# A gradient kernel at the DMA ceiling: scheduler semaphores in place of a critical section, and the last two stores on the queue of the loads

## Chip, cores, metric

One core of a Trainium2 chip. The metric is device time in microseconds of the whole program. The kernel before takes 1248.62 us (median of three runs, 1247.94 to 1251.06).

## The reference

```python
# x: float32 [8192, 8192]
np.gradient(x, axis=1)
# inside a row: (x[j+1] - x[j-1]) / 2 ; at its two ends: x[1]-x[0] and x[m-1]-x[m-2]
```

268.44 MB are read and 268.44 MB written, with one subtraction and one halving per element.

## The kernel before

Rows are handled in 32 sets of 256 (128 partitions times two rows, 8.39 MB). Three slots hold a set each. A set is loaded 64 columns to the right of where its result goes, so that one VectorE pass can work in place. GpSimd first puts the four row-end values aside; the pass covers 16382 columns; a small copy places the row ends; a store sends the set out.

```python
with tc.tile_critical():            # all semaphores by hand
    ...
    def load(i):
        k = i % NB
        if i >= NB:
            nc.sync.wait_ge(ld[(i - 1) % NB], 16 * ld_n[(i - 1) % NB])   # load before has landed
            nc.sync.wait_ge(st[k], 16 * st_n[k])                         # slot has been stored
        nc.sync.dma_start(out=slots[k][:, SH : SH + W], in_=x_sets[i]).then_inc(ld[k], 16)
    ...
    for i in range(nsets):
        at = put_aside(i)                                   # GpSimd
        if i < nsets - 1:
            at = halve(b, 1, W - 1, at)                     # VectorE, 16382 columns
            at = place(nc.scalar if i % 2 else nc.vector, ...)
            store(nc.scalar, i, 0, W, at, st[k])            # ACT queue
        else:                                               # last set in four quarters
            for q in range(PIECES):
                at = halve(b, c0 + 1 - right, c1 - right, at)
                put = place(nc.scalar, ...)
                store(nc.sync, i, c0, c1, put, st_last[q])  # SP queue
        if i + NB < nsets:
            load(i + NB)
    # ... SP waits for all stores
```

## Time and profile before

| what | kernel before |
|---|---|
| median time | 1248.62 us |
| span of the profiled run | 1247.0 us |
| VectorE busy | 554.4 us, 44% |
| bytes and mean rate | 536.88 MB, 431 GB/s |
| last load: issued, landed | 1177.1, 1216.1 us |

How to read it: the page gives the span, the busy time of each engine, the share of DMA engines in use in 40 slices and the chain that ended last. "Stretches" are rows of start:end in us, length, busy time of each engine (number of instructions), the TensorE clock, DMA share, GB/s. The *period* is the mean distance between load issues from the seventh load (near 209 us) to the last, 25 steps; 16.78 MB at the ceiling of 434.3 GB/s take 38.63 us. *Lost DMA time* is worked out from the packet records: the bytes of each packet are spread over its duration, and what is missing from 434.3 GB/s is turned into microseconds, a mean over the 16 engines. The lines of the page, the stretches and the timeline are shown in the prediction.

### The profile page before, as it was taken

The numbers are of one execution on the slowest core, as the hardware profiler recorded it, in microseconds if no ns is written. First come the engines' busy times: TensorE is split into PE (matmuls) and PEld (weight loads), VectorE is DVE, ScalarE is ACT, GpSimd is POOL, SyncE is SP. The second block draws the span as 40 slices with busy tenths as digits, with TensorE's granted clock in tenths as the row PEclk, the third lists the DMA queues.
The fourth block names the chain that finished last, engine by engine and source line by source line (L and its number), as shares of the span: only waits on it lengthen the run. The fifth ranks groups of instructions, "written<-read, shape, count | busy, mean of one in ns | idle before, by whom it ended". The sixth has DMA issues, their size and how long they took to land.

```text
span 1247.0 us, 259 instructions
## 1 busy us (share of the span) xinstructions
DVE 554.4 (44%) x51; ACT 5.0 (0%) x20; POOL 6.5 (1%) x36
## 2 busy tenths in 40 slices
DVE  2841552355533555334553345533455433554335
ACT  0000000000000000000000000000000000000000
POOL 0000000000000000000000000000000000000000
DMA  9999999999999999999999999999999999999998
GB/s 404 437 435 435 412 431 437 435 437 437 437 431 435 435 431 423 435 435 437 433 435 437 437 437 433 431 423 433 435 435 437 435 437 433 435 423 437 435 418 360
DMA packets 9649, 536.88 MB, mean 431 GB/s; under 512 B 1072, under 2 KB 1072, under 8 KB 1072
## 3 DMA queue, kind: packets, MB, share of 16 engines
q1 hardware_dynamic: 5184, 276.83, 51.6%
q10 hardware_dynamic: 4464, 260.05, 48.1%
q14 instruction: 1, 0.01, 0.0%
HBM read 268.44 MB, written 268.44 MB: 431 GB/s over the span
## 4 chain that ended last, share of the span: by engine, by line
DMA 96%; DVE 3%; issue 0%; POOL 0%; ACT 0%; SPq 0%
DMA slot<-in_x_dram 93%; DMA out_dram<-slot 3%; DVE slot L90 3%; POOL ends L78 0%; ACT slot L104 0%; DVE slot L104 0%; SPq L163 0%; SPq L68 0%; SPq L44 0%
## 5 line engine op out<-in xcount | busy, mean ns | idle before, releaser
L90 DVE CUSTOM_DVE_ANT_0 slot<-slot 128x16382 f32<-128x16382 f32 (+1 forms) x35 | 551.6, 15761 | 679.2 <-POOL ends L78 679.1
L78 POOL TENSOR_TENSOR ends<-slot 128x4 f32<-128x4 f32 x32 | 6.3, 198 | 1209.6 <-DMA slot<-in_x_dram 1209.6
L104 ACT COPY slot<-ends 128x4 f32<-128x4 f32 (+1 forms) x19 | 3.7, 197 | 1188.4 <-DVE slot L90 1188.4
L104 DVE COPY slot<-ends 128x4 f32<-128x4 f32 x16 | 2.7, 172 | 0.5
L104 ACT ACT_TABLE_LOAD x1 | 1.3, 1283 | 41.0 <-DVE slot L104 41.0
L152 POOL MEMSET const-uint8-127<- 128x1 uint8 x1 | 0.1, 102 | 0.0
L152 POOL MEMSET const-bfloat16-1.0<- 128x1 bf16 x1 | 0.1, 101 | 0.0
L152 POOL MEMSET const-float32-0.0<- 128x1 f32 x1 | 0.1, 98 | 0.2 <-issue 0.2
L152 POOL MEMSET const-float32-1.0<- 128x1 f32 x1 | 0.1, 98 | 0.0
## 6 DMA issues: line engine op xcount, KB each, us to landing
out_dram<-slot SPq DMA_DIRECT2D x4, 2048.0 KB, 10.1
slot<-in_x_dram SPq DMA_DIRECT2D x32, 38.6
out_dram<-slot ACTq DMA_DIRECT2D x31, 37.8
```

The source lines that it names most:

```text
L78: nc.gpsimd.tensor_sub(out=ends[:, i, :, :], in0=xin[:, :, 1 : m : m - 2], in1=xin[:, :, 0 : m - 1 : m - 2],),
L90: nc.vector._custom_dve(dve_ops.TENSOR_TENSOR_REDUCE_SUB_MAX, out=b[:, c0:c1], in0=b[:, SH + c0 + 1 : SH + c1 + 1], in1=b[:, SH + c0 - 1 : ...
L104: return done(copy(out=out, in_=in_), placed[engine])
L152: nc = _bacc.Bacc("TRN2", target_bir_lowering=False, num_devices=1)
```

## The change

Its intent is that the scheduler sets the semaphores (in program order, with dependences dropped that another wait implies), that the placing copies leave ACT, and that the end runs on one queue: the store of the last set but one goes to SP behind the last load, and the last set goes out in two halves instead of four quarters.

```diff
-    with tc.tile_critical():
-        ld = [nc.alloc_semaphore(f"ld{k}") for k in range(NB)]
-        ... (st, st_last, aside, halved, placed, and their counts)
+    def chain(i, ins, *needed):
+        group, engine = f"slot{i % NB}", ins.ins.engine
+        keep = [o.ins for o in needed]
+        ...
+        tc.declare_no_dep(ins.ins, group=group, keep=keep, reason="implied by the needed step")
+    def load(i):
+        ins = nc.sync.dma_start(out=b[:, SH : SH + W], in_=x_sets[i])
+        if i >= NB:
+            tc.add_manual_dep(ins.ins, loads[-1].ins.name, landed, reason="queue empty")
+        loads.append(chain(i, ins, *([stores[i - NB]] if i >= NB else [])))
+    with tc.manual_schedule():
 ...
-                at = place(nc.scalar if i % 2 else nc.vector, ...)
-                store(nc.scalar, i, 0, W, at, st[k])
-            else:
-                step = W // PIECES                       # four quarters
+            nr = 1 if last else R                        # last set: one row at a time
+            for r in range(0, R, nr):
+                ...
+                placer = nc.gpsimd if i % 5 in (1, 3) and not last else nc.vector
+                queue = nc.scalar if i < nsets - 2 else nc.sync
```

## The prediction

> **What bounds the kernel now.** I read the page first: busy shares, the DMA row in 40 slices, and the chain that ended last.
>
> ```profile
> span 1247.0 us, 259 instructions
> DVE 554.4 (44%) x51; ACT 5.0 (0%) x20; POOL 6.5 (1%) x36
> ...
> DMA  9999999999999999999999999999999999999998
> GB/s 404 437 435 435 412 431 437 435 437 437 437 431 435 435 431 423 435 435 437 433 435 437 437 437 433 431 423 433 435 435 437 435 437 433 435 423 437 435 418 360
> ...
> HBM read 268.44 MB, written 268.44 MB: 431 GB/s over the span
> ...
> DMA 96%; DVE 3%; issue 0%; POOL 0%; ACT 0%; SPq 0%
> ```
>
> VectorE is idle more than half the time; the DMA row is full in every slice and the chain is 96% DMA. The bytes cannot shrink: 268.44 MB in and out are the input and the output once each. The rate sits near 434 in the middle; only the first slice (404) and the last two (418, 360) fall clearly short. Nothing the change does to semaphores, engines or instruction counts in the middle can show unless it leaves the DMA engines without work. So I went to both ends. Next view: stretches with their DMA share and rate.
>
> ```profile
> 0.00:40.00 40.00, 16.86 (x1) 0.00 (x0) 0.40 (x5) 1.00 0.98 419
> 40.00:1180.00 1140.00, 505.04 (x46) 4.25 (x16) 5.94 (x30) 1.00 1.00 433
> ...
> 1222.00:1226.00 4.00, 3.96 (x2) 0.19 (x1) 0.00 (x0) 1.00 0.80 270
> 1226.00:1243.00 17.00, 8.13 (x2) 0.38 (x2) 0.00 (x0) 1.00 1.01 432
> 1243.00:1247.00 4.00, 0.00 (x0) 0.00 (x0) 0.00 (x0) 1.00 0.03 10
> ```
>
> The last two columns are the DMA share and GB/s. For 1140 us the engines have no gap worth naming. There is a hole at 1222 to 1226 and nothing moves in the last 4 us. Third view, the end of the timeline:
>
> ```profile
> 1177.10 0.33 SPq L69 DMA_DIRECT2D slot<-in_x_dram  x1
> ...
> 1177.38 17.22 DVE L90 CUSTOM_DVE_ANT_0 slot<-slot 128x16382 f32<-128x16382 f32 x1 [21.40 <-POOL ends L78]
> 1194.64 0.17 DVE L104 COPY slot<-ends 128x4 f32<-128x4 f32 x1
> 1194.84 0.34 ACTq L108 DMA_DIRECT2D out_dram<-slot  x1
> 1216.13 0.20 POOL L78 TENSOR_TENSOR ends<-slot 128x4 f32<-128x4 f32 x1 [38.78 <-DMA slot<-in_x_dram]
> 1216.36 17.81 DVE L90 CUSTOM_DVE_ANT_0 slot<-slot 128x4095 f32<-128x4095 f32 x4 [21.55 <-POOL ends L78]
> 1220.82 0.19 ACT L104 COPY slot<-ends 128x1 f32<-128x1 f32 x1 [64.61 <-DVE slot L90]
> 1221.04 13.71 SPq L108 DMA_DIRECT2D out_dram<-slot  x4
> ```
>
> The last load (set 31) is issued at 1177.1 on SP. The store of set 30 is issued at 1194.84 on ACT, so load and store share the engines and the load lands only at 1216.1. Then come four quarter passes, each with a 2 MB store behind it.
>
> I also spread the bytes of each packet record over its duration, microsecond by microsecond (the stretches above count a packet whole where it starts, which blurs 64 KB packets of 2.4 us). The ceiling is 434.3 GB/s. Against it the execution loses 10.7 us: 2.8 before the first load flows; 0.9 at 43 to 48, where the first store starts; 0.64 at 1197 to 1204, where the store of set 30 starts on ACT beside the last load; 0.66 at 1223 to 1225, where that store has run dry and the first quarter store has only just been issued; 3.6 from 1243 to the end; the rest in crumbs of at most 0.25. These are the only microseconds to be had.
>
> **What the Trainium skill says.** "DMA: Bandwidth & Descriptors", section "Issuing engines are not separate DMA queues": transfers issued from SP, ACT or GpSimd all end on the same 16 engines, so moving stores from ACT to SP buys no bandwidth. The trace agrees: 434 GB/s with loads alone on one queue (6 to 40 us, packet records), and also with two queues. The same page, "Queues, rings and completion order": each engine takes a queue's work in ring order and alternates between the queues that have work. That is why a store on SP behind the last load no longer slows that load. The queue totals of this trace don't show the order within a ring, so this is the step that I take from the page. The same page, "Where 436 GB/s comes from", gives a fabric ceiling of 435 GB/s; the measured 434 is that ceiling, so a steady part faster than now is not to be expected. "SBUF — State Buffer", section "Who interferes with whom", says a VectorE operation with two SBUF inputs and a GpSimd operation that reads SBUF exclude each other. Twelve placing copies move to GpSimd, but each waits for the pass before it to end and takes about 0.2 us, while VectorE idles some 21 us after every pass (21.40 above). No collision.
>
> **The change, part by part.**
> 1. Semaphores. The order of instructions shows the same two waits ahead of each load (the load before it landed, the store of its slot landed), plus waits for the reuse of a DMA semaphore, which concern transfers that finished long ago (a store waits for the one four sets earlier). In the steady part 0.
> 2. Placing. The 15 ACT copies of 198 ns and the 16 VectorE copies of 172 ns become 12 on GpSimd and 21 on VectorE (two for the halves of the last set); the ACT table load of 1.28 us at 41 us goes. Each copy delays a store by about 0.2 us on either engine, and stores and loads are already queued. In the steady part 0.
> 3. The critical section. At the start the sequencers pass a second branch and wait of about 0.1 us before the first load at 0.95. At the end SP goes through semaphores and a barrier at 1245.2 to 1245.7 (listed at the line of the critical section) before the closing barrier at 1245.5 to 1246.9. The scheduler's own closing waits take some of that place. I count -0.1 at the start and -0.4 at the end.
> 4. The store of set 30 on SP behind the last load. At 1198 the last load still has 2.34 MB to move by the packet records. In front of the store, at 434 GB/s, that takes 5.4 us: mean finish 1203.4, with some microseconds of spread between engines, so I put its landing at 1204 to 1209 instead of 1216.1. The ring is never empty when the store is appended, so the hole of 0.64 us at 1197 should go: -0.6.
> 5. The last set in two halves. A pass of 8190 elements takes 8.7 us (4.43 for 4095 and 17.22 for 16382 give about 1.05 ns an element and 0.1 fixed). With the landing at 1204 to 1209 the first half store is issued at 1213 to 1218, the second 8.9 us later at 1222 to 1227. Meanwhile the store of set 30 flows 19.3 us (8.39 MB at 434), until about 1222.7, and the first half store another 9.65, until 1232.4. About 2 us pass from issue to the first bytes (0.95 to about 3 at the start), so the first half reaches the engines at 1215 to 1220, 3 us or more before they run dry; the second has 3 to 8 us to spare. The hole at 1223 goes: -0.65. Packets of 32 KB instead of 16 KB run nearer the ceiling (432 against 434 over some 19 us): -0.1.
>
> Sum: -0.1 - 0.4 - 0.6 - 0.65 - 0.1 = -1.85 us. Span 1247.0 - 1.85 = 1245.15. The timed median is 1248.62, so the prediction is 1248.62 - 1.85 = about 1246.8.
>
> **Rivals.**
> (a) Coarser halves expose the pass. If the last load kept its landing near 1216, the first half store would come at 1225.2 and move from 1227, while the store of set 30 runs dry at about 1223: a hole of some 4 us instead of 0.66, giving about 1251. For it: the pass doubles from 4.4 to 8.7 us. Against it: that needs load and store still alternating though both are on one queue.
> (b) One queue is weaker than two, say 425 GB/s over the last 45 us: +1 us, which eats half the gain, about 1247.8. Against: the store of set 30 alone ran at 434 at 1214 to 1222 in the packet records.
> (c) A wait of the scheduler holds back each load by a transfer. If a load had to wait for a later store, the 38.6 us period would open a gap of several microseconds some 28 times: above 1300. Against: the listed waits name only the needed transfers and older ones.
> (d) Nothing but noise: the holes are set by engines that lag and stay, the end overhead is the same: 1248.6.
>
> **Range and chances.** The three runs before spread over 3.1 us, more than the effect. A ceiling on the gain is 0.9 + 0.64 + 0.66 + crumbs of 1.2 + about 1 of the end = some 4.4 us, so 1244 is the best that can be thought of. Rival (a) or half of it gives 1249 to 1251. Range 1244.3 to 1249.4. Two per cent is 25 us: more than all idle DMA time, so faster is close to impossible; slower needs rival (c).
>
> **What would show it.** Right: period of loads still 38.6 us and 433 GB/s between 40 and 1180; the last load landing at 1204 to 1209; its half stores issued before the store of set 30 has ended; no stretch under 0.9 DMA share from 1195 to 1240; the last bytes at about 1241.8 and 3.3 us from there to the end. Wrong: a stretch without traffic at about 1223 to 1227 (a); a lower rate after 1205 (b); a longer load period or new SP waits (c).

## The result

The changed kernel took 1249.19 us (median of six runs, 1248.62 to 1249.95), the kernel before 1248.75 us in the same rounds (six runs, 1247.78 to 1251.06). The ratio is 1.0002 with a 95% interval of 0.9989 to 1.0015. A ratio here is the mean time of one kernel's fast runs over that of the other's of the same rounds, so not quite the ratio of the medians. The time lies inside the predicted range, at its upper edge; the forecast gain of 1.85 us did not show in the times.

The page of the changed kernel, with the lines that answer to those of before:

```profile
span 1247.2 us, 267 instructions
DVE 554.8 (44%) x54; POOL 8.8 (1%) x48
...
GB/s 404 437 435 437 431 420 427 437 437 435 435 431 437 437 429 431 427 429 437 437 435 433 437 420 433 437 435 433 422 427 435 431 435 437 435 425 433 435 427 383
...
DMA 93%; DVE 3%; issue 2%; SPq 0%; POOL 0%; POOLq 0%
```

ACT has no work left. The last slice rose from 360 to 383 GB/s, but the middle has more slices at 420 to 431. The same stretches as before:

```profile
0.00:40.00 40.00, 17.12 (x1) 0.40 (x5) 1.00 0.98 419
40.00:1180.00 1140.00, 504.34 (x49) 8.21 (x42) 1.00 1.00 432
...
1222.00:1226.00 4.00, 3.52 (x2) 0.00 (x0) 1.00 0.89 385
1226.00:1243.00 17.00, 0.00 (x0) 0.00 (x0) 1.00 1.01 438
```

The hole of before (1222 to 1226, 270 GB/s) is gone: the packet records show 433 to 434 in each of these four microseconds; the 385 comes from counting long packets where they start. But 40 to 1180 fell from 433 to 432. One GB/s over 1140 us is 1.1 MB, or 2.6 us at the ceiling; rounding could make as much, so the packet records have to say how much it is: 4.55 us lost between 60 us and the last load's issue, against 1.98 before. The end of the timeline:

```profile
1178.11 0.33 SPq L60 DMA_DIRECT2D slot<-in_x_dram  x1
...
1195.80 30.11 SPq L97 DMA_DIRECT2D out_dram<-slot  x3
1207.63 0.20 POOL L72 TENSOR_TENSOR ends<-slot 128x4 f32<-128x4 f32 x1 [29.31 <-DMA slot<-in_x_dram]
1207.86 8.69 DVE L83 CUSTOM_DVE_ANT_0 slot<-slot 128x8190 f32<-128x8190 f32 x1 [12.09 <-POOL ends L72]
1216.59 0.17 DVE L94 COPY slot<-ends 128x2 f32<-128x2 f32 x1
1216.67 8.68 DVE L83 CUSTOM_DVE_ANT_0 slot<-slot 128x8190 f32<-128x8190 f32 x1
```

The last load now lands 29.5 us after its issue instead of 39.0, and the first half is ready at 1216.8, well before the store in front of it runs out on the engines (1224.5 to 1226.6 by the packet records). The end works as planned. Yet the last load was issued at 1178.1, 1.0 us later than before, although the first went out 0.2 us earlier (0.74 against 0.95).

### The profile page after: what moved, and what is told of

It reads as the page before. It is cut to its first block, busy times and chain, and to the rows that moved or that the text cites. A ratio compares the mean times of both kernels' runs of the same rounds, so it can differ in the third digit from the quotient of the medians.

```text
span 1247.2 us, 267 instructions
## 1 busy us (share of the span) xinstructions
DVE 554.8 (44%) x54; POOL 8.8 (1%) x48
## 4 chain that ended last, share of the span: by engine, by line
DMA 93%; DVE 3%; issue 2%; SPq 0%; POOL 0%; POOLq 0%
DMA slot<-in_x_dram 89%; DMA out_dram<-slot 3%; DVE slot L83 3%; DVE slot L94 0%; SPq L60 0%; POOL ends L72 0%; POOLq L129 0%
## 5 line engine op out<-in xcount | busy, mean ns | idle before, releaser
L94 DVE COPY slot<-ends 128x4 f32<-128x4 f32 (+1 forms) x21 | 3.6, 172 | 0.7
## 6 DMA issues: line engine op xcount, KB each, us to landing
slot<-in_x_dram SPq DMA_DIRECT2D x32, 38.6
```

What stands on the lines that cost most here:

```text
L94: ins = placer.tensor_copy(out=res[:, :, 0 : m : m - 1], in_=ends[:, i, r : r + nr, :])
```

## The experiments

Three theories of where the gain went. **Theory 1**: start, end and closing did give what was forecast, and the middle, which is DMA alone, scatters from run to run by more than that. **Theory 2**: the new waits make each load go out later, and that costs time at every load. The chain of waits does show a later issue, before and then after:

```profile
403.69 38.64 DMA slot<-in_x_dram
442.33 0.02 issue
442.35 38.63 DMA slot<-in_x_dram
```

```profile
441.70 38.56 DMA slot<-in_x_dram
480.27 0.02 issue
480.29 0.02 SPq L60
480.30 0.03 issue
480.33 38.57 DMA slot<-in_x_dram
```

Columns: start, length, what. Before, the next load leaves 0.02 us after the landing, since the wait for the landing stands in the load instruction itself. After, the scheduler put that wait in an instruction of its own ahead and left the wait for the store, long satisfied, in the load: 0.07 us. **Theory 3** came with the second round: the middle loses time because engines that have finished their share of a load find the queue of loads empty until the slowest engine has landed its own. (The packet records speak against this reason, as is shown below.)

The experiments went in three groups, each group on one chip (three chips) and beside runs of the kernel before.

**The kernel before again.** No edit.

> The kernel before once more, for a second trace of it. First profile: 25 periods of the load between 210.06 and 1177.10 us, mean 38.68 us. Theory 1 (the 1.9 us that the changed kernel lost in the middle are scatter): the mean period comes out somewhere between 38.65 and 38.80, with the two traces of one kernel differing by about as much as before and after did (0.07). Theory 2 (the new waits cost something per load): 38.66 to 38.70 again. The time is that of the kernel before, ratio 1.000 within 0.001.

Four runs, three of them at 1249.9 to 1253.8 us and one at 1333; ratio of the fast ones 1.0002 (0.9974 to 1.0029). Period 38.75 us, against 38.68 in the first trace of the same kernel: one kernel's own traces differ by as much as the two kernels did. Also, the hole at 1197 to 1204, 0.64 us in the first trace and a term of the prediction, is not there; the hole at 1223 to 1226 is (0.45 us).

**The changed kernel again.** No edit.

> The changed kernel once more, for a second trace of it. First profile: mean period 38.76 us. Theory 1 (scatter): between 38.65 and 38.80. Theory 2 (new waits): 38.74 to 38.78 again. Both: the last load lands near 1207, no hole at its end; ratio 1.000 within 0.001.

1249.40 us against 1250.38, ratio 0.9986 (0.9966 to 1.0006). Period 38.84 us in the profiled run, which was the slowest of its six (1251.05). That is outside what either theory had said.

**The new end alone**, on the kernel before:

```diff
-                store(nc.scalar, i, 0, W, at, st[k])
+                store(nc.scalar if i < nsets - 2 else nc.sync, i, 0, W, at, st[k])
...
-                for q in range(PIECES):      # quarters, four stores
+                for r in range(R):           # halves, two stores
```

> The kernel before with the new end alone: store of the last set but one on SP, last set in two halves with two stores; critical section, semaphores and ACT placing kept. Theory 1: gains what the end gains and nothing else, -0.6 to -1.4 us, ratio 0.9989 to 0.9996. Theory 2: the same end gain without the loss in the middle, so it beats both kernels by 1 to 2 us, period 38.66 to 38.70. Rival (the new end gains nothing because the engines only finish in another order): ratio 1.000 and the last bytes at the same distance from the last load's issue.

1250.07 us against 1250.38, ratio 0.9994 (0.9976 to 1.0013), as theory 1 has it, but the interval takes in no gain at all. Theory 2 had this kernel beat both others; the changed kernel had 1249.40 in the same rounds. Its period, 38.70 us, fits both theories, but its trace (span 1248.3 us) loses 4.23 us between 60 us and the last load's issue: with the old semaphores, as much as the changed kernel. Its last load landed 31.5 us after its issue.

**The new semaphores and placing with the old end**, on the changed kernel:

```diff
-                queue = nc.scalar if i < nsets - 2 else nc.sync
+                queue = nc.sync if last else nc.scalar      # and four quarter passes and stores
```

> The changed kernel with the old end: four quarter passes, store of the last set but one on ACT; scheduler's semaphores and GpSimd and VectorE placing kept. Theory 1: shorter start and closing, -0.2 and -0.9 us, old holes back: ratio 0.9990 to 1.0000. Theory 2: 1.5 to 2 us lost in the middle less about 1 us from start and closing: ratio 1.0003 to 1.0010, period 38.74 to 38.78.

1249.71 us, ratio 0.9995 (0.9975 to 1.0015). By time it speaks for theory 1. The period of the profiled run, 38.88 us, is long, and its middle lost 6.27 us, but that run (1253.59) was the slowest of six.

**Late loads**, on the kernel before, ten times the delay of the change:

```diff
                 nc.sync.wait_ge(ld[(i - 1) % NB], 16 * ld_n[(i - 1) % NB])
-                nc.sync.wait_ge(st[k], 16 * st_n[k])
+                for _ in range(10):      # nine pairs more, all satisfied
+                    nc.sync.wait_ge(ld[(i - 1) % NB], 16 * ld_n[(i - 1) % NB])
+                    nc.sync.wait_ge(st[k], 16 * st_n[k])
```

> The kernel before with nine further waits on SP that are already satisfied, between the landing of a load and the issue of the next: each next load goes out some 0.4 us later, ten times what the changed kernel adds (0.05 us). Theory 1 (a late load is hidden behind the store in flight, the middle is scatter): period 38.65 to 38.85 and ratio 0.999 to 1.002. Theory 2 (each late load costs): 29 times 0.4 us, so period about 39.1 and ratio about 1.009.

The chain of waits of this kernel:

```profile
219.56 38.02 DMA slot<-in_x_dram
...
258.17 0.04 issue
258.21 38.00 DMA slot<-in_x_dram
...
296.80 0.04 issue
296.84 38.01 DMA slot<-in_x_dram
```

Each load leaves 0.6 us after the landing before it, and then takes 38.0 us instead of 38.6. The delay is absorbed whole: the store in flight keeps the engines busy meanwhile (all 16 have a store packet in flight from 257 to 260 us, at 434 GB/s). The period is 38.70 us. Theory 2 called for 39.1, and with the delay of 0.6 that was really had, for 39.3. It falls by the period of this one trace. The ratio, 1.001 (0.9964 to 1.0056), is too wide to say anything by itself. The profiled run took 1258.16 us and lost most of that early:

```profile
GB/s 401 401 382 411 434 432 432 432 432 434 432 434 434 428 432 426 434 428 434 432 434 434 434 434 434 434 432 434 434 434 434 434 434 434 432 434 434 432 434 351
```

Its third load landed at 91.1 us instead of 79.8, before the first added wait (the fourth load is the first that has them). So a disturbance of 10 us can fall on any run.

**The store of the last set but one back on ACT**, on the changed kernel:

```diff
-                queue = nc.scalar if i < nsets - 2 else nc.sync
+                queue = nc.scalar if i < nsets - 1 else nc.sync
```

> The changed kernel with the store of the last set but one back on ACT, halves kept. If the place behind the last load is what makes the halves affordable: the last load lands near 1217 after its issue near 1178, the first half store is issued near 1226, the engines run dry near 1224 and some 3 us are lost: ratio 1.001 to 1.003 and a stretch near 1224 to 1228 with little traffic. If the queue does not matter: last load lands near 1207, ratio as the changed kernel.

The end of its timeline and its stretches:

```profile
1215.54 0.20 POOL L72 TENSOR_TENSOR ends<-slot 128x4 f32<-128x4 f32 x1 [38.45 <-DMA slot<-in_x_dram]
...
1224.70 9.14 SPq L97 DMA_DIRECT2D out_dram<-slot  x2
```

```profile
1198.00:1222.00 24.00, 6.23 (x1) 0.20 (x1) 1.00 1.00 434
1222.00:1226.00 4.00, 3.97 (x3) 0.00 (x0) 1.00 0.38 164
1226.00:1243.00 17.00, 7.43 (x2) 0.00 (x0) 1.00 1.01 432
```

The load takes 38.7 us to land again, the first half store is issued at 1224.7, and the engines are dry meanwhile: 164 GB/s, 1.74 us lost by the packet records from 1223 to 1228 where I had said some 3. From 1224 to 1225.5 at most four engines have a packet in flight. So the halves are affordable only because the store stands behind the load on one queue; rival (a) of the prediction is what happens without it. By time the ratio is 0.9991 (0.9952 to 1.0029; a sixth run, 1318.64 us, was slow), which shows nothing: a hole of 1.7 us drowns in the scatter.

**Loads that don't wait for each other**, on the changed kernel and on the kernel before:

```diff
-        if i >= NB:
-            tc.add_manual_dep(ins.ins, loads[-1].ins.name, landed, reason="queue empty")
```

```diff
-                nc.sync.wait_ge(ld[(i - 1) % NB], 16 * ld_n[(i - 1) % NB])
```

> The changed kernel without the rule that a load waits for the load before it to land; it waits for the store of its slot alone, so there is nearly always a load queued. Theory 3 (the microseconds lost in the middle are engines that finish their share of a load early and find the load queue empty): the loss in the middle falls from 4 us or more to under 1.5, ratio 0.997 to 0.998. Rival (the rule is needed: loads crowd out stores, slots come free in bursts): slower, ratio 1.001 to 1.01. Theory 1 in its pure form (scatter of the memory): no change.

> The kernel before without that same rule; old end, old semaphores. Theory 3: ratio 0.998 to 0.999, and the changed kernel without the rule is faster than this one by what start, closing and end are worth, 1 to 2 us. Rival: slower, as the kernel above.

The traces bear out what theory 3 forecast: the time lost between 60 us and the last load's issue falls from 2 to 6 us in the traces with the rule (9.45 in the disturbed one of the late loads) to 1.1 and 0.6 us, and the spans are 1244.2 and 1243.6 us. The times don't. With the new end four runs lay between 1244.9 and 1246.2 and two at 1260.2 and 1265.8; with the old end the six ran from 1245.7 to 1262.4. Ratios 0.9981 (0.9925 to 1.0038) and 1.0038 (0.9988 to 1.0088). The first leaves out the run of 1265.8, which counts as slow for being over 1.5% above the fastest; with it the ratio of the means would be about 1.0004, no gain. The kernel before had one run of 1263.9 on this chip, so a disturbance was possible. I repeated both on another chip, with the new end on the old semaphores, and the changed kernel a third time.

> The changed kernel without the rule that loads wait for each other, again. Before: four of six runs at 1244.9 to 1246.2 us, two at 1260 and 1266, on a chip where the kernel before had one of 1264 too. If the long runs are a disturbance from outside, most runs here are at 1244 to 1247 and the kernel before shows long ones as often: ratio 0.996 to 0.998. If the kernel without the rule has a second, slower rhythm of its own, runs of 1256 to 1266 come again while the kernel before has none.

> The kernel before without that rule, again. Disturbance: most runs at 1245 to 1248, ratio 0.997 to 0.999. Own slow rhythm: several runs at 1256 to 1263 as last time.

> The kernel before without that rule and with the new end, old semaphores and critical section. With the middle quiet, the parts can be read one by one in the trace: start and closing as in the kernel before (first load at 0.95 us, about 2 us from the last bytes to the end), end as in the changed kernel. Among undisturbed runs about 1.1 us slower than the changed kernel without the rule, and up to 0.7 us faster than the kernel before without the rule.

> The changed kernel a third time. Theory 1 (start, end and closing give 1.8 us, the middle scatters by 2 to 4 us from run to run): ratio 0.998 to 1.001, mean period of the profiled run between 38.68 and 38.84. Theory 2 (the new scheme loses in the middle every time): period 38.75 or more and ratio 0.9995 to 1.001.

The kernel before stayed within 1248.2 to 1250.9 in eleven runs. Without the rule the new end took 1250.3 to 1261.9 (ratio 1.0057, 1.003 to 1.0084), the old end 1248.6 to 1266.6 (1.0068, 1.002 to 1.0115), the new end on old semaphores 1245.2 to 1264.5 (1.0011, 0.9984 to 1.0038, without the run of 1264.46, which counts as slow; about 1.003 with it). Over all rounds 13 of 30 runs without the rule took over 1258 us, and 4 of 82 with it. So the long runs belong to these kernels far more than to the chip. The rule costs a little in the middle and buys steadiness. One part of a longer run is in the profiled run of the new end (1251.83 us):

```profile
400.00:1200.00 800.00, 363.93 (x34) 5.68 (x29) 1.00 1.00 434
...
1234.00:1242.00 8.00, 0.00 (x0) 0.00 (x0) 1.00 0.84 365
1242.00:1250.00 8.00, 0.00 (x0) 0.00 (x0) 1.00 0.05 20
```

The packet records give 27 GB/s in each microsecond from 1243 to 1248, a sixteenth of 434, with one packet in flight: one engine works off what it still has, alone, for some five microseconds. The sister without the new semaphores had a lucky run, 1245.2 us, without such a tail:

```profile
400.00:1200.00 800.00, 359.40 (x32) 1.97 (x10) 3.97 (x20) 1.00 1.00 434
...
1240.00:1243.30 3.30, 0.00 (x0) 0.00 (x0) 0.00 (x0) 1.00 0.03 10
```

No run of 1258 us or more of these kernels fell on a profile, so what the longest ones do stays open.

**Idle engines or slow packets?** I had read the lost time of the middle as idle engines, but had not checked it. The packet records can tell: at every moment they show how many packets are in flight. Between 60 us and the last load's issue the time in which an engine has no packet in flight comes to 0.11 to 0.14 us, a mean over the engines, in the five traces of the two kernels, and to 0.10 to 0.12 without the rule. So hardly any engine was idle, with the rule or without.

What differs is slow packets. A 64 KB packet takes 2.42 us (median). With the rule 65 to 131 of some 7400 took over 2.6 us, up to 3.8, nearly all of them packets of loads, and what they took beyond the median comes to 1.4 to 3.7 us. Without the rule 5 to 48 did, 0.1 to 1.1 us. With the rule the queue of loads had been empty for about 2.8 us at each issue of a load and that of stores for 3.6 us at each issue of a store (medians). Half to nearly all of that excess belongs to packets that end 1 to 9 us after such an issue, and these windows are 41% of the time. Without the rule neither queue had run empty: in all five traces the median issue came 2 to 3 us before the end of the load in front and 8 to 13 us before the end of the store in front. So the loss goes with queues that run empty and are filled again. Why packets are slow then, no run here shows.

That sister was meant to be read part by part: its first load goes out at 0.94 us, and 1.7 us pass from its last bytes to the end where about 2 were expected. The middle of the three traces loses 1.7, 1.1 and 0.4 us, but from 1240 us to the last bytes they lose 6.9, 3.9 and 1.2. How the sister stands in time to the two other kernels without the rule can't be read from runs that scatter so.

The changed kernel the third time (five runs): 1249.48 us against 1249.66, ratio 0.9997 (0.9985 to 1.0009), period 38.73 us. Theory 2 had wanted 38.75 or more.

**All traces of the two kernels side by side.** Lost DMA time in us, a mean over the engines; the drain is what is lost from 1240 us to the last bytes, while the engines finish one after the other; the closing is the time from the last bytes to the end of the span. The columns and the 1236.2 us that the bytes take at the ceiling add up to the span.

| trace | start, 0 to 6 | first store, 6 to 60 | middle, 60 to last load's issue | end, from there to 1240 | drain | closing | span |
|---|---|---|---|---|---|---|---|
| before, first | 2.84 | 0.95 | 1.98 | 1.44 | 1.41 | 2.15 | 1247.0 |
| before, again | 2.85 | 0.98 | 3.95 | 0.63 | 0.98 | 2.14 | 1247.7 |
| after, first | 2.60 | 1.07 | 4.55 | 0.41 | 1.14 | 1.22 | 1247.2 |
| after, again | 2.64 | 0.85 | 4.38 | 0.32 | 3.36 | 1.22 | 1248.9 |
| after, third | 2.60 | 0.92 | 2.95 | 0.07 | 1.06 | 1.22 | 1245.0 |

Start, end and closing sum to 6.43 and 5.62 before, mean 6.03, and to 4.23, 4.18 and 3.89 after, mean 4.10: 1.93 us saved in the mean, and 1.4 to 2.5 us in every pairing of a trace of before with one of after. That leaves the drain out, which is part of the end too and takes 1.20 us in the mean before and 1.85 after, 3.36 of it in one trace. With it the saving is 1.27 us in the mean and anything from -0.9 to 2.9 in a pairing. The middle takes 2.0 and 4.0 before, and 4.6, 4.4 and 3.0 after: the ranges overlap, and their means differ by 1.0 us the other way. The mean spans are 1247.3 before and 1247.0 after. The three ratios in time average 0.9995, some 0.6 us of gain, none of them clear of 1.

## Why the prediction was right or wrong

**The bound, and two per cent.** Right. The DMA engines are full, and no part of the change touches the bytes. (The prediction read only the first slice of the page and the last two as short. The fifth, 412, is lower than the 418; it lost 0.12 us by the packet records, so nothing hung on it.) The 435 GB/s of "DMA: Bandwidth & Descriptors", section "Where 436 GB/s comes from", held too: full microseconds of the packet records read 434 to 435 GB/s in every trace. That section gives another limit besides; see the list at the end.

**Part 1, semaphores: 0 in the steady part.** Right as far as the wait goes, by the late loads: a delay of 0.6 us per load was absorbed. The prediction missed that the order of the two waits makes each load 0.05 us later; no cost of it shows.

**Part 2, placing: 0.** No sign against it: the store goes out 17.7 to 17.8 us after the landing in both kernels, and no collision of GpSimd and VectorE appears (the waits for GpSimd's copies are for the pass before). It was not tried alone.

**Part 3, start and closing: -0.5.** Too small: the first load leaves 0.21 us earlier, and the closing takes 1.22 us instead of 2.15, together -1.14. I had counted the barrier at the critical section's line, but not that some 0.6 us more pass before the last exchange of semaphores (1245.7 to 1246.3), which has no counterpart after. But that part is not the critical section's by itself: the three kernels that keep it and drop the rule lack this pause, and their closing takes 1.65 to 1.68 us against 1.21 and 1.22 for the two with the scheduler's semaphores and without the rule. That is a difference of 0.45, near the 0.4 that was forecast. Where the other 0.5 comes from stays open.

**Parts 4 and 5, the end: -1.35.** The mechanism was right point by point: landing at 1207.6 within 1204 to 1209 (1209.3 and 1205.4 in the other two traces), half stores ahead of the store's end, no hole at 1223. And the ACT variant shows that the queue is what does it, as the order in one ring would have it, which I took from the Trainium skill ("DMA: Bandwidth & Descriptors", section "Queues, rings and completion order"): with both on SP the load landed after 29.5 us, with the store on ACT after 38.7. The size was off: the mean lost time at the end fell from 1.04 to 0.27, so -0.77. The mis-sized term is the hole at 1197 to 1204, 0.64 us in the one trace that I had and absent from the second. Nor was it a hole: all 16 engines had a packet in flight, but packets of the load took up to 3.6 us instead of 2.4 when the store began. A ring that never runs empty may be the right remedy, but not because engines had lacked work. The first half store was to come 3 us or more before the engines run dry; from the prediction's own ends (1220 against 1222.7) it is 2.7.

**The sum.** -1.85 was forecast for start, end and closing together, and the traces give -1.93. That the two errors cancel is luck; with the drain, which was not forecast to change, it is -1.27.

**What failed** is the step that nothing but the ends moves. The sum was set against one median and the middle taken as constant: "In the steady part 0", because nothing there "can show unless it leaves the DMA engines without work". The middle is not constant: five traces of two kernels lose 2.0 to 4.6 us there, with the engines at work all the while, some of them on slower packets. The prediction's own signs say the same: for a right prediction it named a period of 38.6 us and last bytes at about 1241.8, and the three traces have 38.73 to 38.84 and 1243.8 to 1247.7. In the first pair of traces it took back 2.6 us (4.55 against 1.98), more than the 2.2 that start, end and closing gave, and the spans came out 0.2 us apart; the times, 1249.19 instead of 1246.8, fit that. That the time still fell inside the range is luck: its upper end was set with half of rival (a) in view, and rival (a) did not happen. Rival (d), nothing but noise, described the clock, but for a wrong reason: the hole at 1223 did go. Whether the changed kernel also loses up to a microsecond in the middle by itself stays open. The traces cannot say: with the other kernels that keep the rule, the old semaphores lose 2.0, 4.0 and 4.2 us (the disturbed trace of the late loads aside) and the new ones 3.0 to 6.3. The only candidate named, the later loads, is ruled out by the one trace with late loads.

**Why the middle loses at all.** Shown is that it goes with the rule: without it the loss falls to 0.4 to 1.7 us. The reason is not the one that I had in mind. A load has landed when its slowest engine has; the increments of one load's semaphore come in 0.5 to 0.7 us apart for the first load, but 4.7 and 8.4 us apart (median from the seventh load on) in the two traces of before, and 4.1 to 9.0 in the three of after. The next load is issued only then, so fast engines run out of loads. But they don't idle: they have store packets in flight, and the trace with 8.4 us loses least, 1.98 us. Most of what is lost is lost in slow packets, and half to nearly all of their excess in the microseconds after a queue that had run empty got a new transfer. Without the rule no queue runs empty, and the increments are 1.0 to 3.4 us apart; so the rule does not keep the engines in step either. The cause of the slow packets stays open, and so does the cause of the long runs without the rule.

## What to carry to other kernels

When the DMA engines are full, little is left: the two ends, and the moments at which a queue runs empty. Take at least two traces of each kernel before pricing a loss: one that is in one trace only is not a property of the kernel. Ask of lost time whether engines are idle or packets slow before explaining it. A store that is ready while the last load is in flight belongs behind that load on the same queue: the load lands earlier (here by 9 us), its work hides under the store, and the last set can then be cut more coarsely. In the times, what this is worth could not be told from noise here. A rule that makes loads wait for each other cost a few microseconds in the middle, and without it the runs scattered; judge its removal by many runs, not by the best trace.

## What the Trainium skill lacked or had wrong

- "DMA: Bandwidth & Descriptors", section "Latency and other measured facts", gives about 600 ns to the first byte for transfers from SP or ACT. Here 1.0 us passed from the issue of the first load to its first packet on idle engines, and 3.4 to 4.5 us when a queue that had run empty was filled again while the other queue was moving 64 KB packets (6.1 to 6.4 us for the first store). The page has no first-byte figure for a busy engine; the prediction's "about 2 us from issue to first bytes" was too low for that case.
- The same page, section "Queues, rings and completion order", says that a transfer is spread over engines, and elsewhere that they finish independently. It has no size for how far they drift apart: 4 to 9 us here between the first and the last engine of one 8.39 MB load (medians of the five traces from the seventh load on), and 1.0 to 3.4 us when loads did not wait for each other.
- No page says how far a program scatters that is bound by DMA alone: 2.0 to 4.6 us lost in the middle of 1247 us, with the engines idle for 0.1 us of it, and single runs of the kernel before at 1257 and 1264 us.
- No page has the cost of the closing that the program itself brings along: from the last bytes to the end 1.21 to 1.22 us with the scheduler's semaphores (1.48 with the old end), 1.65 to 2.22 with the critical section.
- "DMA: Bandwidth & Descriptors", section "Where 436 GB/s comes from", says that for transfers between HBM and SBUF the share of HBM, about 358 GB/s, binds. For the one core here it did not: loads alone ran at 434 GB/s (6 to 40 us), and loads with stores too.
